# Query, gate and probability scratch tensors laid out by query block, compressed product last, rope query stores in one piece of 128 rows

## The chip, the cores and the metric

The kernel runs on one core of a Trainium2 chip, as one program and one launch. The metric is the device time of one execution in microseconds. A core has a matmul engine (PE, TensorE, with its weight loads as PEld), a vector engine (DVE), an activation engine (ACT), a general engine (POOL, GpSimd) and a queue engine (SP, SyncE) that issues nearly all transfers between DRAM and the on-chip memory. 16 DMA engines carry those transfers. PE writes its results to PSUM banks; DVE and ACT take them from there.

## The reference, cut to what matters

A trunk of two layers over a sequence of 1024 tokens. The second ("odd") layer mixes two attentions, and only its parts are touched here. NSA has 8 query heads on 2 key heads and adds three branches: compressed keys, selected blocks, and a window; MLA has 8 heads with a 64-wide plain part and a 32-wide rope part.

```python
def nsa_mixer(q, kv, gate_logits, ...):
    p_c = masked_softmax(s_c, dist_c >= 0)                       # compressed branch
    o_cmp = jnp.einsum('bygsc,bcyd->bsygd', p_c, vc)
    _, sel_idx = lax.top_k(sel_score, n_top)                     # blocks for the selected branch
    ...                                                          # o_sel, o_win by blocks of 128 queries
    o = g[:, :, 0] * o_cmp + g[:, :, 1] * o_sel + g[:, :, 2] * o_win

def mla_mixer(c_q, c_kv, k_rope, ...):
    q = (rms_norm(c_q, q_norm) @ w_uq).reshape(bsz, s_len, 8, 64 + 32)
    q = concat([q[..., :64], rope(q[..., 64:], positions)], -1)
    return einsum(masked_softmax(q @ k.T * scale), v)            # per head, causal

def odd_mixer(...):
    y_c = nsa_mixer(...) * jax.nn.silu(g_n)
    y_d = mla_mixer(...) * jax.nn.silu(g_m)
    return concat([y_c, y_d]) @ w_out
```

## The kernel before

All matrix products run on PE. A float32 operand is split into a high and a low part ("hi", "lo"), and three products are summed (`mm3`). A projection gives a PSUM tile `S` of 128 features x 1024 tokens (two of these exist, "banks" below); ACT and DVE take it out.

The second layer (`layer1`) runs these stages. `query_proj` makes the NSA queries: per head one tile `hp` of 128 rows (64 hi, 64 lo) x 1024 tokens, stored to `q_dram` (L1140). `cmp_attn` is the compressed branch in eight steps of 128 queries: softmax on DVE and ACT, then the probabilities, transposed, as `pcT` to `pc_dram` (L1191), and from step 4 on the block selection, stored as `sel_dram` (L1220). `gate_proj` makes the two gates (L1231, L1232) and stores them to `gn_dram` and `gm_dram` (L1233). `mla_q` makes the MLA queries in two rope parts (c = 0, 1: L1429 to L1438) and four plain parts (L1445 to L1451); both rope parts work in the same two halves of the tile `cst` (t1, t2), so that the second part may write them only when the stores of the first have landed. The rope store (L1438) goes to `qr_dram` as 4 heads x 32 rows x 1024, three times: hi, hi, lo.

Then `nsa` takes the query blocks of 128 in the order 1, 2, 0, 3, 4, 5, 6, 7. Its `load` brings a block's queries (L1299, L1301), the slope rows (L1302, on POOL), the selection rows (L1304), and gate and compressed probabilities into one tile `sgpc` (L1306, L1307). Two query slots are filled ahead, so the loads of the third block (i = 0) wait until the first block's last product has read its slot. Per block there are two head pairs `gp`; for each, one PSUM tile `o` (a single one exists) collects the compressed product (L1322), then the window and the selected branch (scores L1340, L1345, softmax L1241 to L1253, transposes L1265, products L1360), and `store_y` (L1280) takes it out. `mla` does the same for 16 steps of MLA; `mla_load` brings its queries (L1517, L1520, L1522).

The code is written in program order, and a scheduler of the framework decides in which order each engine's queue holds the instructions; so moving one statement changes the order of others. SP works its queue strictly in order. In the DRAM layouts of before, a tensor has one row per feature over all 1024 tokens, and a load of one block of 128 tokens therefore picks pieces of 128 float32 = 512 bytes; the stores write whole rows of 4 KB.

Of the kernel before, what the change touches and what calls it, by code (L numbers as in the profile page):

```python
# [6 lines left out]
F32 = mybir.dt.float32  # L7
# [15 lines left out]
class Trunk:  # L23
# [1127 lines left out]
    def cmp_attn(self):  # L1151
# [3 lines left out]
        self.pc_dram = self.dram.tile([8, 128, 4, 128], F32, name="pc_dram")  # L1155
# [11 lines left out]
        for i in range(8):  # L1167
# [23 lines left out]
            nc.sync.dma_start(self.pc_dram[i], pcT)  # L1191
            if i >= 4:
# [24 lines left out]
                sl = self.t4([2, 4, 128], F32R, name="sl")[0:16]  # L1217
                src = pt[0:16, 0:256].rearrange("p (y o t) -> p y o t", y=2, o=1).to_broadcast([16, 2, 4, 128])
                nc.scalar.copy(sl, src)
                nc.sync.dma_start(self.sel_dram[i - 4].bitcast(F32), sl.rearrange("p y g t -> p (y g) t").bitcast(F32))  # L1220
            yield

    def gate_proj(self, dst, cols):

        nc = self.nc
        for c2 in range(2):
            wt = self.wchunk(*cols(2 * c2), *cols(2 * c2 + 1))
            for cc in range(2):
# [4 lines left out]
                nc.sync.dma_start(dst[2 * c2 + cc], th)  # L1233
# [51 lines left out]
    def nsa(self):  # L1285
# [7 lines left out]
        src = self.q_dram.rearrange("h p t -> p h t")  # L1293

        def load(step):
# [10 lines left out]
            nc.sync.dma_start(sp[:, 0], self.gn_dram[:, :, ts].rearrange("g p t -> p g t"))  # L1306
            nc.sync.dma_start(sp[:, 1], self.pc_dram[i])  # L1307
# [6 lines left out]
        for step, i in enumerate(order):  # L1314
# [4 lines left out]
            for gp in range(2):  # L1319
                o = self.ps_o.tile([128, 2, 128], F32, tag="o", name="o")  # L1320
                for y in range(2):
                    nc.tensor.matmul(o[64 * y:64 * y + 64].rearrange("p g t -> p (g t)"), self.vc[64 * y:64 * y + 64],  # L1322
                                     pcT[64 * y:64 * y + 64, 2 * gp:2 * gp + 2].rearrange("p g t -> p (g t)"),
                                     start=True, stop=False, skip_group_check=True)
                for br, (KA, KB) in ((1, self.Kwin), (0, self.Ksel)):
# [5 lines left out]
                    for s0 in range(0, 4, hg):  # L1331
                        S = self.bank2().rearrange("p (h n) -> p h n", h=hg)
                        for s_ in range(hg):
                            y, g2 = divmod(s0 + s_, 2)
                            hd = 4 * y + 2 * gp + g2
# [22 lines left out]
                    for kt in range(nk):  # L1358
                        for y in range(2):
# [3 lines left out]
                                             start=False, stop=(br == 0 and kt == nk - 1), skip_group_check=True)  # L1363
# [32 lines left out]
    def mla_q(self):  # L1396
# [43 lines left out]
        for c in range(4):  # L1440
# [9 lines left out]
            for b in range(2):  # L1450
                nc.sync.dma_start(dst[192 * b:192 * b + 64], hi[64 * b:64 * b + 64].bitcast(F32))  # L1451
# [222 lines left out]
```

## Time and profile before

| what | value |
|---|---|
| three runs before | 1593.4, 1596.39, 1603.84 us; median 1596.39 |
| the profiled execution, its own time | 1592.17 us |
| its span in the trace | 1590.1 us |
| PE busy | 1475.7 us, 93% of the span |
| DVE, ACT, POOL busy | 993.7, 633.3, 369.5 us |
| chain that ended last | PE 70%, DVE 17%, issue 4%, DMA 3% |
| mean granted TensorE clock | 0.969 of full speed |

The profile is one execution. The span runs from the first to the last instruction; the execution's own time is 2.1 us longer. Times within the trace are counted from the span's start. A "releaser" is what ended an engine's idle time. The granted clock is given as a share of 2.4 GHz; 0.50 is the lower level, 1.2 GHz.

### The profile page before, as it was taken

The page shows a single profiled execution, that of the slowest core. Times are in us where ns is not written, and L with a number is a line of the kernel's source. Part 1 is how long each engine was busy: PE and PEld are TensorE (multiplying, and loading weights), DVE is VectorE, ACT ScalarE, POOL GpSimd, SP SyncE. Part 2 cuts the span into 40 slices and gives each one's busy share as a digit, 9 for nine tenths or more (in the row PEclk, how much of TensorE's full clock was granted, in tenths as well). Part 3 has the DMA queues.
Part 4 walks back from the last instruction along what each step waited for, and adds up shares of the span by engine and source line. Part 5 has one row for each costly group of instructions (what it writes and reads, how often), then busy time and mean ns, then how long its engine had stood idle before and what let it go on. Part 6 is the DMA issues. An engine that isn't in the chain of part 4 may idle for free.

```text
span 1590.1 us, 22273 instructions
## 1 busy us (share of the span) xinstructions
PE 1475.7 (93%) x8284; PEld 1176.6 (74%) x8284; DVE 993.7 (62%) x2168; ACT 633.3 (40%) x1293; POOL 369.5 (23%) x324
## 2 busy tenths in 40 slices
PE   4799999969899999999999979999999999998998
PEld 4597787757787788789877756666666777786787
DVE  6899999967544654661386336767775677544322
ACT  5332121247422343431253216767666666412211
POOL 4527733340323301410321300000001100223300
PEclk8899999979999999999999989999999999999999
DMA  8012453322522521542733246212113341532421
GB/s 251 14 53 81 126 180 131 127 73 79 184 99 80 179 98 66 148 144 82 185 92 103 77 133 192 70 51 61 36 45 89 86 124 52 149 110 80 160 86 69
DMA packets 144349, 168.65 MB, mean 106 GB/s; under 512 B 19817, under 2 KB 111713, under 8 KB 144241
## 3 DMA queue, kind: packets, MB, share of 16 engines
q1 hardware_dynamic: 139536, 155.83, 31.6%
q0 software_dynamic: 4544, 11.38, 2.5%
q8 instruction: 66, 1.08, 0.3%
q14 instruction: 43, 0.34, 0.1%
q10 hardware_dynamic: 160, 0.01, 0.0%
HBM read 114.20 MB, written 50.99 MB: 104 GB/s over the span
## 4 chain that ended last, share of the span: by engine, by line
PE 70%; DVE 17%; issue 4%; DMA 3%; ACT 2%; SPq 2%; POOL 2%; ACTq 0%; POOLq 0%; DVEq 0%
PE S L114 38%; PE tr L1265 7%; PE o L1360 5%; DVE conv L264 5%; PE tr L114 3%; PE o L1562 3%; PE S L1345 2%; PE S L1340 2%; PE S L1553 1%; PE S L1550 1%; PE tr L802 1%; PE S L1554 1%; PE S L1270 1%; SPq L1301 1%; PE tr L973 1%
## 5 line engine op out<-in xcount | busy, mean ns | idle before, releaser
L114 PE MATMUL S<-xT,wt 128*128 128x512 f32 x768 | 188.3, 401 | 4.2 <-DVE ext L249 4.2
L114 PE MATMUL S<-X,wt 128*128 128x512 f32 x768 | 185.2, 396 | 6.0 <-ACT wt L107 2.3
L114 PE MATMUL S<-wg,hT 128*128 128x512 f32 x720 | 176.8, 402 | 10.3 <-ACT wg L107 4.5
L114 PE MATMUL S<-wo,Y 128*128 128x512 f32 x768 | 181.5, 395 | 4.9 <-DVE gb L688 3.5
L114 PEld LDWEIGHTS S<-xT,wt 128*128 128x128 f32 x768 | 144.9, 192 | 35.6 <-DVE ext L249 5.0
L114 PEld LDWEIGHTS S<-X,wt 128*128 128x128 f32 x768 | 142.9, 189 | 37.4 <-issue 4.0
L114 PEld LDWEIGHTS S<-wo,Y 128*128 128x128 f32 x768 | 143.9, 189 | 35.8 <-DVE gb L688 3.9
L114 PEld LDWEIGHTS S<-wg,hT 128*128 128x128 f32 x720 | 136.7, 193 | 42.9 <-ACT wg L107 7.6
L1241 DVE TENSOR_REDUCE nm<-S 128x1 f32<-128x640 f32 (+7 forms) x132 | 129.2, 980 | 54.4 <-PE S L1345 34.4
L264 DVE SCALAR_TENSOR_TENSOR conv<-ext,conv 128x1024 f32<-128x1024 f32 x116 | 148.9, 1284 | 2.3
L108 POOL TENSOR_TENSOR wt<-raw,wt 128x1024 fp32r<-128x1024 f32 x34 | 82.5, 2442 | 115.4 <-ACT wt L107 115.2
L1244 ACT ACTIVATE pslot<-S,nm 128x640 f32<-128x640 f32 (+7 forms) x128 | 89.8, 709 | 25.6 <-DVE nm L1241 14.6
L1266 ACT COPY PT<-tr 128x512 f32<-128x512 f32 (+3 forms) x172 | 80.1, 491 | 45.6 <-PE tr L1265 42.5
L1265 PE MATMUL tr<-ident,pslot 128*128 128x128 f32 x528 | 84.7, 284 | 0.0
L1360 PE MATMUL o<-PT,vslot 128*64 128x256 f32 x528 | 84.5, 391 | 0.0
L1265 PEld LDWEIGHTS tr<-ident,pslot 128*128 128x128 f32 x528 | 58.6, 142 | 29.8 <-issue 20.8
L97 DVE TENSOR_SCALAR rs_v<-ss 128x1 f32<-128x1 f32 x32 | 4.9, 153 | 119.1 <-ACT lh L93 99.3
L1345 PE MATMUL S<-kst,qslot 112*128 112x512 f32 (+3 forms) x192 | 73.7, 396 | 0.0
L1340 PE MATMUL S<-kst,qslot 128*128 128x512 f32 (+3 forms) x192 | 69.7, 363 | 2.3 <-ACT pslot L1244 1.4
L787 POOL TENSOR_TENSOR lh<-lh 128x1024 f32<-128x1024 f32 x16 | 39.9, 2495 | 119.4 <-DVE lh L786 96.7
L93 ACT ACTIVATE lh<-S 128x1024 f32<-128x1024 f32 x16 | 16.4, 1026 | 123.6 <-issue 95.0
L852 DVE SCALAR_TENSOR_TENSOR ov<-ov,S 128x1024 f32<-128x1024 f32 (+1 forms) x17 | 19.7, 1157 | 72.3 <-issue 44.6
(433 smaller groups left out, 2812.5 us busy)
## 6 DMA issues: line engine op xcount, KB each, us to landing
h_dram<-lh POOLq DMA_DIRECT2D x16, 512.0 KB, 3.2
hr<-h_dram SPq DMA_DIRECT2D x14, 512.0 KB, 3.3
raw<-ev_w_in SPq DMA_DIRECT2D x16, 256.0 KB, 4.8
raw<-ev_w_in SPq DMA_DIRECT2D x8, 512.0 KB, 6.7
raw<-ev_w_out SPq DMA_DIRECT2D x8, 512.0 KB, 4.5
t<-ple_gate SPq DMA_DIRECT2D x8, 512.0 KB, 6.0
raw<-ple_gate SPq DMA_DIRECT2D x8, 512.0 KB, 5.9
lh<-x SPq DMA_DIRECT2D x8, 512.0 KB, 3.9
```

The source lines that it names most:

```text
L108: (eng or self.nc.gpsimd).tensor_tensor(lo, raw, hi, OP.subtract)
L114: self.nc.tensor.matmul(ps, l, r, start=n == 0, stop=n == len(seq) - 1)
L264: nc.vector.scalar_tensor_tensor(out=last if s == 30 else acc, in0=src, scalar=wc, in1=acc, op0=OP.mult, op1=OP.add)
L787: nc.gpsimd.tensor_tensor(hv, hv, xr, OP.add)
L1241: nc.vector.tensor_reduce(out=nm[:, 0:hg], in_=S[:, :, 0:n], op=OP.max, axis=AX.X, negate=True)
L1244: nc.scalar.activation(out=P[:, h, 0:n], in_=S[:, h, 0:n], func=AF.Exp, bias=nm[:, h:h + 1], accum_out=sm[:, h:h + 1])
L1265: nc.tensor.transpose(ps[:, c:c + 128], P[:, h, 128 * (k0 + k):128 * (k0 + k) + 128], self.ident)
L1266: nc.scalar.copy(PT[:, k0:k0 + n, s0:s0 + hg], ps[:, 0:128 * n * hg].rearrange("p (k h t) -> p k h t", h=hg, t=128))
L1340: nc.tensor.matmul(o_, QA[:, hd], KA[:, y, ks], start=True, stop=False)
L1345: nc.tensor.matmul(o_, qb[:, hd], KB[:, y, ks], start=False, stop=True)
L1360: nc.tensor.matmul(o[64 * y:64 * y + 64].rearrange("p g t -> p (g t)"), self.vsw[:, k0 + kt, 128 * br + 64 * y:128 * br + 64 * y + 64], PT ...
L1562: nc.tensor.matmul(o[64 * b:64 * b + 64, q], vm[:, kt, vs], PT[:, kt, 2 * b + q], start=(kt == 0), stop=(kt == nk - 1))
```

## The change

Four DRAM tensors get the query block i as first index: `q_dram` is [block, row, head, 128] instead of [head, row, 1024], `qm_dram` [block, half, row, head, 128], `gm_dram` [block, half, row, 2, 128], and `gp_dram` [block, row, 2, 4, 128] takes the place of `gn_dram` and `pc_dram`. A block's load then reads whole rows of 1, 2 or 4 KB, and the stores write pieces of 512 bytes. The heads are ordered by the half they belong to, so that the loads of halves are contiguous too; the slope rows come in two POOL transfers instead of one, the selection rows are stored in two halves from a tile of half the width, and gate and probabilities of a block come in one transfer. The plain MLA queries are stored in 16 transfers of 64 rows instead of 4 of 128 and 8 of 64. The rope queries are stored as 128 rows x 4 KB, once hi and once lo, and each MLA step reads them in three transfers of 32 rows. In `nsa` the compressed product comes after both branches instead of before.

```diff
@@ query_proj
-        self.q_dram = self.dram.tile([8, 128, 1024], F32R, name="q_dram")
+        self.q_dram = self.dram.tile([8, 128, 8, 128], F32R, name="q_dram")
...
-                    nc.sync.dma_start(self.q_dram[hd].bitcast(F32), A.bitcast(F32))
+                    nc.sync.dma_start(self.q_dram[:, :, 4 * b + c].rearrange("i p t -> p i t").bitcast(F32),
+                                      A.rearrange("p (i t) -> p i t", i=8).bitcast(F32))
@@ cmp_attn
-            nc.sync.dma_start(self.pc_dram[i], pcT)
+            nc.sync.dma_start(self.gp_dram[i, :, 1], pcT)
...
-                sl = self.t4([2, 4, 128], F32R, name="sl")[0:16]
+                sl = self.t4([2, 2, 128], F32R, name="sl")[0:16]
...
+                for b in range(2):
+                    nc.sync.dma_start(self.sel_dram[i - 4, :, 4 * b:4 * b + 4].bitcast(F32),
+                                      sl.rearrange("p y g t -> p (y g) t").bitcast(F32))
@@ gate_proj
-                nc.sync.dma_start(dst[2 * c2 + cc], th)
+                nc.sync.dma_start(dst(2 * c2 + cc), th.rearrange("p (i t) -> p i t", i=8))
@@ nsa, load
-            nc.sync.dma_start(QA.bitcast(F32), src[:, :, ts].bitcast(F32))
+            nc.sync.dma_start(QA.bitcast(F32), self.q_dram[i].bitcast(F32))
             for b in range(2):
-                nc.sync.dma_start(qb[0:64, b:8:2].bitcast(F32), src[64 * b:64 * b + 64, b:8:2, ts].bitcast(F32))
-            nc.gpsimd.dma_start(qb[64:66], d["c_qaug"][:, :, ts])
+                hs = slice(4 * b, 4 * b + 4)
+                nc.sync.dma_start(qb[0:64, hs].bitcast(F32), self.q_dram[i, 64 * b:64 * b + 64, hs].bitcast(F32))
+                nc.gpsimd.dma_start(qb[64:66, hs], d["c_qaug"][:, b:8:2, ts])
...
-            nc.sync.dma_start(sp[:, 0], self.gn_dram[:, :, ts].rearrange("g p t -> p g t"))
-            nc.sync.dma_start(sp[:, 1], self.pc_dram[i])
+            nc.sync.dma_start(sp, self.gp_dram[i])
@@ nsa, per head pair
-                for y in range(2):
-                    nc.tensor.matmul(o[64 * y:64 * y + 64]..., self.vc[64 * y:64 * y + 64], pcT[...], start=True, stop=False)
...
-                                             start=False, stop=(br == 0 and kt == nk - 1), skip_group_check=True)
+                                             start=(br == 1 and kt == 0), stop=False, skip_group_check=True)
+                for y in range(2):
+                    nc.tensor.matmul(o[64 * y:64 * y + 64]..., self.vc[64 * y:64 * y + 64], pcT[...], start=False, stop=True)
@@ mla_q
-        self.qr_dram = self.dram.tile([8, 96, 1024], F32R, name="qr_dram")
+        self.qr_dram = self.dram.tile([2, 2, 128, 1024], F32R, name="qr_dram")
...
-            for r, s in ((0, hi), (32, hi), (64, lo)):
-                nc.sync.dma_start(self.qr_dram[4 * c:4 * c + 4, r:r + 32].bitcast(F32), s.bitcast(F32))
+            for a, s in enumerate((hi, lo)):
+                nc.sync.dma_start(self.qr_dram[c, a].bitcast(F32), s.bitcast(F32))
...
             for b in range(2):
-                nc.sync.dma_start(dst[192 * b:192 * b + 64], hi[64 * b:64 * b + 64].bitcast(F32))
+                pr = slice(64 * b, 64 * b + 64)
+                dst = self.qm_dram[:, c // 2, :, 2 * b + c % 2].rearrange("i p t -> p i t").bitcast(F32)
+                for rows, s in ((pr, hi), (slice(64 - 64 * b, 128 - 64 * b), lo)):
+                    nc.sync.dma_start(dst[rows], s[pr].rearrange("p (i t) -> p i t", i=8).bitcast(F32))
@@ mla_load
-        nc.sync.dma_start(QR.bitcast(F32), self.qr_dram[hs, :, ts].rearrange("h p t -> p h t").bitcast(F32))
+        for r, a in ((0, 0), (32, 0), (64, 1)):
+            src = self.qr_dram[u, a, :, ts].rearrange("(h r) t -> r h t", h=4)
+            nc.sync.dma_start(QR[r:r + 32].bitcast(F32), src.bitcast(F32))
```

How the change moves instructions, as the built programs hold them. A row gives the line, the operation, the tile written and read, the shape, and a count. In the changed program the lines are some higher (L1442 is the rope store, L1301 and L1304 the query loads, L1309 the `sgpc` load, L1338 the first score product, L1363 the compressed product, L1456 the plain query store).

First, SP's queue where `mla_q`'s first rope part (`cst`) is stored and the first two query blocks (`qslot`, `sgpc`) are loaded, before:

```order
L1438 DMA qr_dram<-cst 4x32x1024 x3
L1299 DMA qslot<-q_dram 128x8x128
L1301 DMA qslot<-q_dram 64x4x128 x2
L1299 DMA qslot<-q_dram 128x8x128
L1301 DMA qslot<-q_dram 64x4x128 x2
L1306 DMA sgpc<-gn_dram 128x4x128
L1307 DMA sgpc<-pc_dram 128x512
```

The same place in the changed program:

```order
L1442 DMA qr_dram<-cst 128x1024
L1301 DMA qslot<-q_dram 128x1024
L1304 DMA qslot<-q_dram 64x512
L1442 DMA qr_dram<-cst 128x1024
L1304 DMA qslot<-q_dram 64x512
L1301 DMA qslot<-q_dram 128x1024
L1304 DMA qslot<-q_dram 64x512 x2
L1309 DMA sgpc<-gp_dram 128x1024 x2
```

Two rope stores stand where three stood, and the lo store has moved behind the first two loads.

Second, PE's queue between the last gate projection (`X`, `wt`) and the first NSA scores (`kst`, `qslot`); `Cq`, `wuq` is the MLA query projection, 12 rows to each of its parts. Before:

```order
L114 MATMUL S<-X_4694,wt 128x512 x4
L114 MATMUL S<-X_4695,wt 128x512 x4
L114 MATMUL S<-Cq,wuq 128x512 x36
L1322 MATMUL o<-sgpc,vc 64x256 x2
L114 MATMUL S<-Cq,wuq 128x512 x36
L1340 MATMUL S<-kst,qslot 128x256
```

Changed:

```order
L114 MATMUL S<-X_4694,wt 128x512 x4
L114 MATMUL S<-X_4695,wt 128x512 x4
L114 MATMUL S<-Cq,wuq 128x512 x72
L1338 MATMUL S<-kst,qslot 128x256
L1273 LDWEIGHTS mbf
L1273 MATMUL S<-mbf 128x128
```

The compressed product of the first head pair has left the middle of the MLA projection.

Third, SP's queue where the plain MLA queries (`hps`) are stored, ahead of the loads of the third query block, in the changed program:

```order
L1456 DMA qm_dram<-hps 64x8x128 x2
L1442 DMA qr_dram<-cst 128x1024
L1456 DMA qm_dram<-hps 64x8x128 x2
L1442 DMA qr_dram<-cst 128x1024
L1456 DMA qm_dram<-hps 64x8x128 x12
L1304 DMA qslot<-q_dram 64x512
L1301 DMA qslot<-q_dram 128x1024
```

Before, the same stretch held eight stores of 64 rows x 4 KB, four of 128 rows x 4 KB and three rope stores; the load of the third block stood behind them too.

## Rows read from the trace of the kernel before

**Rows 1.** Page, section 1: busy time, share, instructions of the engines.

```profile
PE 1475.7 (93%) x8284; PEld 1176.6 (74%) x8284; DVE 993.7 (62%) x2168; ACT 633.3 (40%) x1293; POOL 369.5 (23%) x324
```

**Rows 2.** Busy by stretch; the last three: granted clock, DMA share, GB/s.

```profile
core 0: us, PE busy (x) PEld busy (x) DVE busy (x) ACT busy (x) POOL busy (x), PEclk, DMA share, GB/s
918.00:934.00 16.00, 16.00 (x72) 13.14 (x70) 4.88 (x4) 2.09 (x2) 3.33 (x6) 1.00 0.35 113
934.00:946.00 12.00, 5.70 (x14) 3.80 (x12) 3.74 (x4) 1.06 (x2) 0.00 (x0) 0.72 0.49 151
946.00:962.00 16.00, 11.34 (x46) 8.64 (x47) 4.73 (x4) 3.49 (x4) 0.00 (x0) 0.79 0.59 182
968.00:980.00 12.00, 12.00 (x79) 8.70 (x78) 8.97 (x27) 9.08 (x31) 1.11 (x4) 0.86 0.78 221
980.00:1200.00 220.00, 220.00 (x1492) 143.73 (x1492) 160.28 (x386) 154.48 (x394) 7.44 (x14) 1.00 0.22 60
1260.00:1380.00 120.00, 118.85 (x992) 93.62 (x991) 80.44 (x164) 77.56 (x171) 10.53 (x7) 1.00 0.36 105
```

**Rows 3.** PE in order of time: start, duration, instruction, idle before and its releaser.

```profile
928.69 5.66 PE L114 MATMUL S<-Cq,wuq 128*128 128x512 f32 x24
939.33 5.36 PE L114 MATMUL S<-Cq,wuq 128*128 128x512 f32 x12 [4.99 <-DVE cst L1429]
950.66 1.12 PE L1322 MATMUL o<-sgpc,vc 64*64 64x256 f32 x4 [5.96 <-DMA sgpc<-pc_dram]
951.71 9.84 PE L114 MATMUL S<-Cq,wuq 128*128 128x512 f32 x36
961.39 0.28 PE L1340 MATMUL S<-kst,qslot 128*128 128x256 f32 x1
...
998.59 0.31 PE L1340 MATMUL S<-kst,qslot 128*128 128x128 f32 x1
```

**Rows 4.** DVE and ACT in order of time, the MLA query parts.

```profile
929.95 1.22 DVE L1232 SCALAR_TENSOR_TENSOR th<-th,S 128x1024 f32<-128x1024 f32 x1 [7.13 <-ACT th L1231]
938.05 1.22 DVE L1429 TENSOR_TENSOR cst<-S,cst 128x1024 f32<-128x1024 f32 x1 [6.88 <-DMA qr_dram<-cst]
943.45 1.22 DVE L1431 TENSOR_TENSOR cst<-S,cst 128x1024 f32<-128x1024 f32 x1 [4.17 <-DMA qr_dram<-cst]
944.73 1.02 ACT L1445 ACTIVATE hps<-S 128x1024 fp32r<-128x1024 f32 x1 [14.82 <-PE S L114]
```

**Rows 5.** SP's queue in order of time: start, time the issue took.

```profile
921.58 3.01 SPq L1438 DMA_DIRECT2D qr_dram<-cst  x3
924.70 3.87 SPq L1299 DMA_DIRECT2D qslot<-q_dram  x1
928.62 11.16 SPq L1301 DMA_DIRECT2D qslot<-q_dram  x2
...
954.27 1.13 SPq L1451 DMA_DIRECT2D qm_dram<-hps  x2
...
982.44 2.27 SPq L1301 DMA_DIRECT2D qslot<-q_dram  x1
```

**Rows 6.** Stretches, columns as in rows 2: rope stores; 4 KB; 512 B stores.

```profile
932.00:940.00 8.00, 3.01 (x13) 2.15 (x12) 1.22 (x1) 0.00 (x0) 0.00 (x0) 0.85 0.27 106
740.00:744.00 4.00, 4.00 (x21) 3.31 (x19) 1.23 (x1) 0.83 (x2) 0.00 (x0) 1.00 0.65 262
164.00:165.00 1.00, 1.00 (x6) 0.83 (x5) 1.00 (x3) 0.00 (x0) 0.39 (x1) 1.00 0.92 278
```

**Rows 7.** Transfers: count, KB each, median us from issue to landing.

```profile
CA_dram<-s5c SPq DMA_DIRECT2D x16, 128.0 KB, 2.4
gm_dram<-th SPq DMA_DIRECT2D x4, 512.0 KB, 2.6
```

**Rows 8.** POOL in order of time, and the slope rows' transfers from 915 to 960.

```profile
924.71 1.25 POOL L1302 DMA_DIRECT2D qslot<-c_qaug  x2
...
qslot<-c_qaug POOLq DMA_DIRECT2D x2, 8.0 KB, 8.7
```

**Rows 9.** ACT in order of time, with SP's query stores of that place.

```profile
796.25 1.98 ACT L107 CAST wt<-raw 128x1024 fp32r<-128x1024 f32 x2
798.25 1.02 ACT L1120 ACTIVATE hp<-S 64x1024 fp32r<-64x1024 f32 x1
...
791.71 6.24 SPq L1140 DMA_DIRECT2D q_dram<-hp  x3
```

**Rows 10.** Line L1522, the rope query loads of `mla`, and `store_y`'s L1280.

```profile
L1522 SPq DMA_DIRECT2D qmslot<-qr_dram x16: 543/544/601, 1187.0 to 1334.5; - x16
DMA to landing us min/median/max: 2.7/3.0/3.6
...
L1280 DVE SCALAR_TENSOR_TENSOR yt<-o,sgpc x16: 416/424/425, 977.7 to 1212.7; 128x256 f32<-128x256 f32 x16
```

**Rows 11.** Tile `sl`, the selection rows' copy on ACT.

```profile
L1219 ACT CAST sl<-tr x4: 1002/1002/1002, 854.5 to 892.4; 16x1024 fp32r<-16x1024 f32 x4
```

More of the change, by code (lines that the diff above doesn't have):

```diff
@@ L1154, in cmp_attn @@
         nc, d, V = self.nc, self.d, self.nc.vector
-        self.pc_dram = self.dram.tile([8, 128, 4, 128], F32, name="pc_dram")
         self.sel_dram = self.dram.tile([4, 16, 8, 128], F32R, name="sel_dram")
@@ L1334, in nsa @@
                             y, g2 = divmod(s0 + s_, 2)
-                            hd = 4 * y + 2 * gp + g2
+                            hd = 4 * g2 + 2 * y + gp
                             for c in range(0, n, 512):
@@ L1362, in nsa @@
                                              PT[:, kt, 2 * y:2 * y + 2].rearrange("p g t -> p (g t)"),
-                                             start=False, stop=(br == 0 and kt == nk - 1), skip_group_check=True)
+                                             start=(br == 1 and kt == 0), stop=False, skip_group_check=True)
+                for y in range(2):
+                    nc.tensor.matmul(o[64 * y:64 * y + 64].rearrange("p g t -> p (g t)"), self.vc[64 * y:64 * y + 64],
+                                     pcT[64 * y:64 * y + 64, 2 * gp:2 * gp + 2].rearrange("p g t -> p (g t)"),
+                                     start=False, stop=True, skip_group_check=True)
                 if i == 7 and gp == 0:
@@ L1423, in mla_q @@
         yield
-        self.qm_dram = self.dram.tile([8, 128, 1024], F32R, name="qm_dram")
-        self.qr_dram = self.dram.tile([8, 96, 1024], F32R, name="qr_dram")
+        self.qm_dram = self.dram.tile([8, 2, 128, 4, 128], F32R, name="qm_dram")
+        self.qr_dram = self.dram.tile([2, 2, 128, 1024], F32R, name="qr_dram")
         for c in range(2):
@@ L1536, in mla @@
             sgm = self.t2([2, 128], name="sgm")
-            nc.sync.dma_start(sgm, self.gm_dram[2 * u:2 * u + 2, :, ts].rearrange("g p t -> p g t"))
+            nc.sync.dma_start(sgm, self.gm_dram[i, u])
             hg = self.group_size(n)
@@ L1549, in mla @@
                         o_ = S[:, s_, ks]
-                        nc.tensor.matmul(o_, QA[:, h4], KA[:, h4, ks], start=True, stop=False)
+                        nc.tensor.matmul(o_, QA[:, s0 + s_], KA[:, h4, ks], start=True, stop=False)
                         if c + m == n:
                             self.add_mask(S[:, s_, n - 128:n], self.mask_diag)
-                        nc.tensor.matmul(o_, QB[:, h4], KB[:, q, ks], start=False, stop=False)
+                        nc.tensor.matmul(o_, QB[:, s0 + s_], KB[:, q, ks], start=False, stop=False)
                         nc.tensor.matmul(o_, QR[:, h4], KR[:, ks], start=False, stop=True)
@@ L1571, in layer1 @@
         w = self.d["od_w_in"][0]
-        self.gn_dram = self.dram.tile([4, 128, 1024], F32, name="gn_dram")
-        self.gm_dram = self.dram.tile([4, 128, 1024], F32, name="gm_dram")
+        self.gp_dram = self.dram.tile([8, 128, 2, 4, 128], F32, name="gp_dram")
+        self.gm_dram = self.dram.tile([8, 2, 128, 2, 128], F32, name="gm_dram")
         self.compress_in()
@@ L1587, in layer1, with gn, gm @@
         self.key_stacks()
-        for dst, cols in ((self.gn_dram, lambda k: [w[:, 1304 + 256 * y + 64 * k:1304 + 256 * y + 64 * k + 64]
-                                                    for y in range(2)]),
-                          (self.gm_dram, lambda k: [w[:, 2232 + 128 * k:2232 + 128 * k + 128]])):
-            if dst is self.gm_dram:
+        def gn(k):
+            return self.gp_dram[:, :, 0, k].rearrange("i p t -> p i t")
+        def gm(k):
+            return self.gm_dram[:, k // 2, :, k % 2].rearrange("i p t -> p i t")
+        for dst, cols in ((gn, lambda k: [w[:, 1304 + 256 * y + 64 * k:1304 + 256 * y + 64 * k + 64] for y in range(2)]),
+                          (gm, lambda k: [w[:, 2232 + 128 * k:2232 + 128 * k + 128]])):
+            if dst is gm:
                 mq = self.mla_q()
@@ L1595, in layer1 @@
                 next(cmp, None)
-                if dst is self.gm_dram and k in (2,3):
+                if dst is gm and k in (2,3):
                     next(mq)
```

14 lines of the change are left out of this document (3 added, 11 removed).

## The prediction

> **What bounds the kernel now.** I read the busy table first: PE is busy 93% of the span, no other engine over 62% [rows 1]. So a change counts where PE waits or runs slowly, and I looked for that by stretches. In the NSA stage (980 to 1200) PE is busy 220.00 of 220 us at full clock, in the main part of MLA 118.85 of 120 [rows 2]: there a faster transfer has nothing to give. Between 934 and 962, though, PE is busy only 5.70 of 12 and 11.34 of 16 us, at clock 0.72 and 0.79 [rows 2]. This is the passage from the last gate to the first NSA scores, and every part of the change meets in it.
>
> The order of time on PE shows two waits there [rows 3]. At 934.35 (928.69 + 5.66) PE has done both products of the second rope part and wants a free bank; it waits 4.99 us for L1429 on DVE. At 944.69 it has done the first plain part and comes to the compressed product L1322; it waits 5.96 us for the load of `pc_dram`. Behind each wait the clock is down: 12 products take 5.36 us where 24 took 5.66 before.
>
> What is late behind the two waits? L1429 starts at 938.05, after 6.88 us of waiting for the rope stores, and L1431 waits for them again [rows 4]. SP's queue says the same: it hands out three rope stores at 921.58, then the first query load takes 3.87 us to issue and the next two 11.16 us [rows 5]; the `sgpc` loads stand behind these. While SP hangs, the 16 DMA engines are only 27% busy and move 106 GB/s [rows 6], about a quarter of them. So it is not a shortage of bandwidth: the rope store, whose target begins with 4 heads, runs on about 4 engines. Three stores of 0.524 MB at 106 GB/s are 14.8 us, 921.6 to 936.4, close to where L1429 is let go.
>
> **The change part by part, here.** Rope stores: two instead of three, and 128 rows of 4 KB like the gate's store, which lands in 2.6 us [rows 7]. Issued at 921.6, hi has landed by about 924.2; lo is issued behind two loads, by about 925, and has landed by 928. Both are far ahead of DVE's needs (931.5, 934.4). Now the passage again, with 2.83 us for 12 products at full clock (half of 5.66), 1.02 us on ACT and 1.22 on DVE for each part [rows 3, 4]:
> the first rope product ends at 931.5, DVE has finished with the gate (929.95 + 1.22), L1429 runs 931.5 to 932.8, and its bank is free when PE asks at 934.35. Plain part 0 runs to 937.2, part 1 to 940.0. Part 2 needs the bank of part 0: ACT to 938.2, DVE to 939.4, in time; it runs to 942.8. Part 3 needs the bank of part 1: ACT to 941.0, DVE (behind the rope lo) to 942.3, in time; it runs to 945.6. The first scores need the bank of part 2: 942.8 + 1.02 + 1.22 = 945.1. So they start at 945.6 where they started at 961.39 [rows 3]: 15.8 us. By terms: 4.99 and 5.96 of waiting, 1.12 of the products L1322 that leave this place, 5.36 - 2.83 = 2.5 and 9.84 - 8.49 = 1.35 of half clock, 15.9 together.
>
> The products L1322 are moved, not removed. They come back inside the NSA stage, where PE has no gap: between 0.6 (half of 1.12, at full clock) and 1.12 us; I take 0.6. What remains is 15.2 us.
>
> Do the loads keep up with a start 15.8 us earlier? Two query blocks and two `sgpc` are 2 x (0.524 + 2 x 0.131) + 2 x 0.524 = 2.6 MB, with the rope stores 3.7 MB. At the rate of 4 KB rows (262 / 0.65 = 403 GB/s) that is 9 us, at that of 512 B pieces (278 / 0.92 = 302 GB/s) 12 us [rows 6]: done by 931 to 934, against 945.6. The slope rows are four POOL transfers instead of two: issued from 924.71 in 2.5 us instead of 1.25, landing 8.7 us later [rows 8], 936. Cover 10 us; without it each us late would be a us lost.
>
> **The other parts.** Stores in 512 B pieces: 0.524 MB takes 1.74 us instead of 1.30 by the two rates, 0.44 more. For the eight gate stores nothing waits (DMA share 0.35 and less around them [rows 2]). Of the query stores, three at 791.71 are slow already (6.24 us) and ACT's next `hp` at 798.25 reuses a buffer of the first [rows 9]; it could start 0 to 1.3 us later. I take 0. The selection copy is half as wide; four of 1.00 us [rows 11] give between 0 and 2 us on ACT. PE's waits in that stretch end on DVE, so I take 0.
>
> Plain query stores: 16 of 64 rows in 512 B pieces instead of 12, the same 4.19 MB. In SP's order the loads of the third block stand behind them. They begin at about 938 instead of 954.27; before, they and three rope stores kept SP until 982.44 [rows 5], 28 us. Even with 28 us the load starts at 966 and lands near 970; PE wants it at 998.59 - 15.8 = 982.8 [rows 3]. Cover 12 us: nothing.
>
> The compressed product last: `o` becomes free one product later, since `store_y` (0.42 us [rows 10]) can only follow it. A group's first product then comes at most 0.6 + 0.42 = 1.0 us too early, 16 times: 0 to 16 us. In the new queue two to eight transposes and mostly new scores stand between L1363 and the next group's first product, so I take 0.
>
> MLA: three rope loads of 32 rows a step instead of one: two more issues of 0.54 us on SP, landing 3.0 us [rows 10]. A step is over 7 us (120 us for some 14 steps [rows 2]), SP idles most of it, and the loads run a step ahead: nothing. The `qm`, `gm` and query loads in longer rows save DMA time that nobody waits for.
>
> **Sum.** 1592.2 - 15.8 + 0.6 = 1577.0 us against the profiled execution, a ratio of 0.990. That execution is 4.2 us below the median of the runs shown and 1.2 below the lowest. With the ratio the median 1596.4 becomes 1581.2. I forecast between the two: 1579 us.
>
> **Rivals.**
> *A wait stays in the passage* (1582 to 1587). If anything still holds PE 3 us at 934 (the rope lo, the bank order), the clock goes down again and part 0 costs 2.5 us more: 5.5 us less gain, 1582.5 on the profiled execution's scale, up to 1587 on that of the runs. For it: three engines have to mesh within a margin of 0.3 to 1.6 us, as worked out above. Against: all of these margins are small only beside PE work, and a miss costs its own size.
>
> *The NSA order costs what the passage gives* (1583 to 1592). The scheduler has reordered the whole stage. If `o` really stands between the groups, the 1.0 us of each of 16 groups returns and the time is 1592. For it: PE had no gap, so each new one is loss. Against: DVE is busy 160 and ACT 154 of 220 us [rows 2], so both have room, and the amount of work is the same.
>
> *The plain query stores come late* (slower, 1593 to 1612). A store of 64 rows and 128 KB lands in 2.4 us when alone [rows 7]; twice the bytes take at most 4.8. One after another, 16 would take 77 us, from 938 to 1015, the load of block 0 would land at 1018 instead of 982.8, and PE would wait 35 us: 1577 + 35 = 1612. It decides from (982.8 - 3.3 - 938) / 16 = 2.6 us for each store; at 3.6 us the whole gain is gone. Against: the 28 us above are a bound of 2.3 us for each twelfth part of the same bytes, with rope stores on top, at 221 GB/s [rows 2].
> The Trainium skill ("DMA: Bandwidth & Descriptors", section "Rules for kernel authors") speaks for this rival: two transfers to disjoint halves of the partitions serialize, and one transfer of 128 should be used instead; by it the sixteen halves would run as sixteen transfers in a row, which is the case just priced. No run here shows two such halves apart; I give it the small chance that the 28 us leave.
>
> *More comes back* (1570 to 1574). The clock of 968 to 980 is 0.86 [rows 2], 1.7 us; with the 2 us of the selection copy the time is 1573. Against: the fill of the softmax pipeline that lowers the clock there stays.
>
> **How the numbers follow.** Forecast 0.61 (its own range 1574 to 1584), a wait stays 0.14, the NSA order 0.13, late stores 0.06, more 0.06. The range 1570 to 1590 leaves out the late stores and the worst of the NSA order, about 0.1. A change of about 1% is what a measurement of this kernel can tell from none, here 1580.4 against 1596.4. The forecast lies on this border: I put 0.65 of it below (0.40), and with the case "more" faster has 0.46. Slower is the late stores, 0.06. The rest, 0.48, is within 1%.
>
> **What would show it.** Right: no wait of PE for L1433 (the old L1429) nor for `sgpc`, the first scores near 946, the clock 1.00 from 918 on, DMA share well over 0.27 while rope stores run, SP's query loads issued in under 1 us each; NSA still 220 us from block 1's end to block 7's. Wrong: PE waiting at the scores of the third block on `qslot` (the late stores), PE gaps before a group's first L1358 (the NSA order), or a first score near 950 (a wait stays).

## The result, and the profile after

The changed kernel takes 1579.34 us (median; 1576.96 to 1583.41) where the kernel before takes 1594.99 beside it (four runs, three of them those shown ahead of the prediction). The ratio on record is 0.9877, interval 0.9844 to 0.9911; the quotient of the two medians, 0.9902, lies inside it. Measured once more beside the last experiments it is 0.9892 (0.9863 to 0.992). The profiled execution takes 1576.96 us with a span of 1575.2.

The stretches of [rows 2] again, after (columns as there; the last one holds work that stood some 15 us later before):

```profile
core 0: us, PE busy (x) PEld busy (x) DVE busy (x) ACT busy (x) POOL busy (x), PEclk, DMA share, GB/s
918.00:934.00 16.00, 16.00 (x72) 13.18 (x71) 6.79 (x6) 2.09 (x2) 4.35 (x8) 1.00 0.80 237
934.00:946.00 12.00, 12.00 (x55) 9.86 (x54) 7.25 (x6) 4.03 (x4) 0.00 (x0) 1.00 0.80 242
946.00:962.00 16.00, 13.72 (x92) 10.73 (x92) 11.34 (x24) 10.33 (x36) 1.63 (x5) 0.89 0.91 232
980.00:1200.00 220.00, 218.46 (x1501) 145.36 (x1500) 155.87 (x363) 152.44 (x382) 13.95 (x22) 1.00 0.19 54
```

From 934 to 946 PE is now busy 12.00 of 12 us at clock 1.00 (before: 5.70 at 0.72), and the DMA share from 918 to 946 is 0.80. The order of time on PE, which answers to [rows 3]:

```profile
918.87 11.05 PE L114 MATMUL S<-X,wt 128*128 128x512 f32 x48
929.75 16.59 PE L114 MATMUL S<-Cq,wuq 128*128 128x512 f32 x72
946.18 0.28 PE L1338 MATMUL S<-kst,qslot 128*128 128x256 f32 x1
...
948.72 0.38 PE L1338 MATMUL S<-kst,qslot 128*128 128x256 f32 x1 [0.92 <-DVE hps L1450]
...
951.81 0.38 PE L1338 MATMUL S<-kst,qslot 128*128 128x256 f32 x1 [1.37 <-ACT pslot L1247]
...
959.27 0.42 PE L1338 MATMUL S<-kst,qslot 128*128 128x384 f32 x1
```

All six remaining query parts (72 products) run in one piece, and the first scores follow at 946.18. SP's queue, after, which answers to [rows 5]:

```profile
922.66 0.34 SPq L1442 DMA_DIRECT2D qr_dram<-cst  x1
923.60 0.34 SPq L1301 DMA_DIRECT2D qslot<-q_dram  x1
...
925.70 1.26 SPq L1301 DMA_DIRECT2D qslot<-q_dram  x1
927.01 1.36 SPq L1304 DMA_DIRECT2D qslot<-q_dram  x2
928.42 1.06 SPq L1309 DMA_DIRECT2D sgpc<-gp_dram  x2
...
941.63 2.85 SPq L1456 DMA_DIRECT2D qm_dram<-hps  x2
...
945.87 14.46 SPq L1456 DMA_DIRECT2D qm_dram<-hps  x12
960.43 1.02 SPq L1304 DMA_DIRECT2D qslot<-q_dram  x1
```

The first two `sgpc` loads are out by 929.48; the plain query stores keep SP until 960.33, and the load of block 0 follows at once, 22 us before PE comes to that block's scores (982.78). On DVE the first rope product of the second part waits for PE alone, no longer for a transfer as in [rows 4]:

```profile
932.68 1.23 DVE L1433 TENSOR_TENSOR cst<-S,cst 128x1024 f32<-128x1024 f32 x1 [0.44 <-PE S L114]
935.45 1.23 DVE L1435 TENSOR_TENSOR cst<-S,cst 128x1024 f32<-128x1024 f32 x1 [1.54 <-PE S L114]
```

**How the runs are compared.** Single executions of one kernel lie up to 15 us apart (e4: 1586.98 to 1602.38 in ten runs; before: 1591.72 to 1605.34 in 22). In the traces much of that comes ahead of the change: the last gate product, a run of 48 products, starts at 914.84 in one trace and at 922.05 in another of kernels whose code is the same up to there (e11, e6). The passage behind it, from the start of that product to the first NSA scores, repeats to 0.02 us in four profiles (the changed kernel twice, e8, e9); each kernel in which PE waits there has one profile. So each profile is cut into three: the start of that product, the passage, and what is left from the first scores to the end of the span (us). The ratio in the last column is to runs of the kernel before beside it.

| kernel | gate product starts | passage | rest | time as a ratio to before |
|---|---|---|---|---|
| before | 917.78 | 43.61 | 628.71 | 1 |
| changed | 918.87 | 27.31 | 629.02 | 0.9877 (0.9844 to 0.9911) |
| changed, again | 923.61 | 27.31 | 630.68 | 0.9892 (0.9863 to 0.992) |
| e1 before, rope store of 128 rows | 917.21 | 29.90 | 630.99 | 0.9914 (0.9882 to 0.9947) |
| e2 before, compressed product last | 915.29 | 35.27 | 631.84 | 0.9952 (0.9925 to 0.9978) |
| e3 block layout alone | 918.54 | 42.64 | 629.02 | 0.9962 (0.994 to 0.9983) |
| e4 changed, old rope store | 921.63 | 34.63 | 638.84 | 0.9978 (0.9954 to 1.0002) |
| e5 changed, compressed product first | 916.04 | 28.19 | 628.57 | 0.9904 (0.9883 to 0.9926) |
| e6 before, two pieces of 4 x 32 | 922.05 | 41.75 | 627.10 | 0.9981 (0.9963 to 0.9999) |
| e7 before, three pieces of 128 | 920.84 | 28.16 | 629.00 | 0.9891 (0.9871 to 0.991) |
| e8 changed, query stores of 128 rows | 914.45 | 27.29 | 630.16 | one execution, 1573.65 us |
| e9 changed, one rope load a step | 919.61 | 27.29 | 631.10 | 0.9891 (0.9859 to 0.9922) |
| e10 changed, last query part between scores | 917.45 | 24.56 | 629.99 | 0.985 (0.9821 to 0.988) |
| e11 before, rope stores from ScalarE's queue | 914.84 | 42.90 | 629.26 | 0.9982 (0.9964 to 1.0) |

In e10 one query part of 2.7 us stands behind the first scores, so its passage is shorter by that without a gain.

### The profile page after: what moved, and what is told of

It reads as the page before. It is cut to its first block, busy times and chain, and to the rows that moved or that the text cites. A ratio compares the mean times of both kernels' runs of the same rounds, so it can differ in the third digit from the quotient of the medians.

```text
span 1575.2 us, 22336 instructions
## 1 busy us (share of the span) xinstructions
PE 1467.4 (93%) x8284; PEld 1172.2 (74%) x8284; DVE 998.9 (63%) x2168; ACT 631.0 (40%) x1293; POOL 372.9 (24%) x332
## 4 chain that ended last, share of the span: by engine, by line
PE 67%; DVE 20%; issue 4%; ACT 3%; DMA 2%; POOL 2%; SPq 1%; ACTq 0%; POOLq 0%; DVEq 0%
PE S L114 37%; DVE conv L264 7%; PE tr L1268 6%; PE o L1358 5%; PE tr L114 3%; PE o L1568 2%; PE S L1343 2%; PE S L1338 2%; PE S L1559 1%; PE S L1556 1%; PE tr L802 1%; PE S L1560 1%; PE S L1273 1%; PE tr L973 1%; DVE s5a L507 1%
## 5 line engine op out<-in xcount | busy, mean ns | idle before, releaser
L1268 PEld LDWEIGHTS tr<-ident,pslot 128*128 128x128 f32 x528 | 58.4, 142 | 24.9 <-issue 19.6
L1338 PE MATMUL S<-kst,qslot 128*128 128x512 f32 (+3 forms) x192 | 69.7, 363 | 3.5 <-ACT pslot L1247 2.5
L852 DVE SCALAR_TENSOR_TENSOR ov<-ov,S 128x1024 f32<-128x1024 f32 (+1 forms) x17 | 19.7, 1157 | 72.1 <-issue 44.6
```

Of the source, the lines that this page charges most:

```text
L1268: nc.tensor.transpose(ps[:, c:c + 128], P[:, h, 128 * (k0 + k):128 * (k0 + k) + 128], self.ident)
L1338: nc.tensor.matmul(o_, QA[:, hd], KA[:, y, ks], start=True, stop=False)
```

## The experiments: one part of the change at a time

**e1, the rope store alone.** The kernel before, with

```diff
-            for r, s in ((0, hi), (32, hi), (64, lo)):
-                nc.sync.dma_start(self.qr_dram[4 * c:4 * c + 4, r:r + 32].bitcast(F32), s.bitcast(F32))
+            for a, s in enumerate((hi, lo)):
+                nc.sync.dma_start(self.qr_dram[c, a].bitcast(F32), s.bitcast(F32))
...
```

The lines that lay `qr_dram` out and load it to match are left out here, and in e6 and e7 below.

> The kernel before with one part of the change: the rope query store in two pieces of 128 rows, loaded in three pieces of 32 rows. Theory (the shape of the rope store causes both waits of the passage, the second one because it keeps SP's queue shut in front of the loads of queries and gates): both waits go, the first NSA scores start near 946 instead of 961.4, the time falls by 14 to 16 us, to about 1580 where the kernel before has 1595. Rival A (the second wait has its own cause, the product that stands first and the load it needs): only 4.99 us and 2.5 us of half clock go, the second wait of some 6 us stays, about 1587.

PE in order of time, e1:

```profile
928.11 5.62 PE L114 MATMUL S<-Cq,wuq 128*128 128x512 f32 x24
935.50 0.65 PE L1322 MATMUL o<-sgpc,vc 64*64 64x256 f32 x4 [1.77 <-DMA sgpc<-pc_dram]
936.08 11.19 PE L114 MATMUL S<-Cq,wuq 128*128 128x512 f32 x48
947.11 0.28 PE L1340 MATMUL S<-kst,qslot 128*128 128x256 f32 x1
```

13.7 of the 16.3 us come from this part alone. The first wait is gone, the second shrinks from 5.96 to 1.77 us: it hung on the rope store, not on a cause of its own. What is left of it goes with the order: the scheduler put the compressed product behind 24 products here, where 36 stood ahead of it before [rows 3]. In e7 below, with 36 ahead again, it waits for nothing.

**e2, the compressed product alone** (the two products L1322 behind both branches, `start` on the first product of the window branch).

> The kernel before with one part of the change: the compressed product behind both branches. Theory: the wait for the rope store stays (4.99 us, half clock behind it); the wait of 5.96 us for the gates leaves PE, which fills it with the plain query parts until about 954; first scores near 954 to 955, 0.6 us come back in the NSA stage: about 1589. Rival A (each wait has its own cause): about the same, 1588 to 1589, which makes e1 the run that decides. Rival B (the block layout opens the queue): PE meets the query loads next, 1593 to 1595.

The wait for L1429 stays, and the passage is 8.3 us shorter (PE in order of time, e2):

```profile
936.65 4.96 PE L114 MATMUL S<-Cq,wuq 128*128 128x512 f32 x12 [4.83 <-DVE cst L1429]
942.26 8.46 PE L114 MATMUL S<-Cq,wuq 128*128 128x512 f32 x36 [0.65 <-DVE cst L1431]
950.56 0.28 PE L1336 MATMUL S<-kst,qslot 128*128 128x256 f32 x1
```

**e3, the block layout alone** (the changed kernel with the old rope store and the old place of the product).

> The changed kernel without its rope store (three pieces of 4 x 32 rows again, one load of 96 rows) and with the compressed product first again: what is left is the block layout of queries, gates and probabilities. Theory: next to nothing, since SP is still shut behind the rope stores: 1593 to 1596, PE still waits some 5 us for the first rope part and some 5 us for the gates. Rival B (longer rows in the loads open SP's queue): the waits of SP on the query loads (3.87 and 11.16 us) shrink, 1582 to 1587.

Both waits stay, and the passage is only 1.0 us shorter (PE, then SP's queue):

```profile
939.97 5.43 PE L114 MATMUL S<-Cq,wuq 128*128 128x512 f32 x12 [4.88 <-DVE cst L1433]
949.51 1.12 PE L1324 MATMUL o<-sgpc,vc 64*64 64x256 f32 x4 [4.11 <-DMA sgpc<-gp_dram]
```

```profile
929.48 2.96 SPq L1304 DMA_DIRECT2D qslot<-q_dram  x2
...
938.59 5.23 SPq L1309 DMA_DIRECT2D sgpc<-gp_dram  x2
```

The half of rival B that speaks of SP came true: the six query loads take SP 9.2 us to hand out instead of 19.7 (the pair at 929.48 takes 2.96 instead of 11.16). Its gain did not: the `sgpc` loads go out at 938.59 and take 5.23 us themselves, and the gates are there 31.0 us behind the start of the gate product instead of 32.9 (949.51 - 918.54, 950.66 - 917.78). By time e3 is 0.9962, with an interval below 1, 4.6 us between the medians; 1.0 us of that lies in the passage, and where the rest lies the runs do not show. e2 and e3 together with e1 add up to 23 us where the whole change has 16.3: they are different ways around the same obstacle.

**e4, the changed kernel without its rope store** (the three pieces of 4 x 32 rows again).

> The changed kernel with only the rope store as it was (three pieces of 4 x 32 rows, one load of 96 rows). Theory: as e2, the first wait and its half clock are back, the second is not: 1588 to 1590, 9 to 10 us over the changed kernel. Rival A: the same 1587 to 1589. Rival B (the block layout carries the gain): 1579 to 1582.

The passage is 7.3 us longer than the changed kernel's, as expected, but the rest is 8 to 10 us longer too, and the gain is all but gone (0.9978). SP and PE say why (SP's queue; PE; the stretch behind PE's wait, columns as in [rows 2]):

```profile
956.79 3.69 SPq L1442 DMA_DIRECT2D qr_dram<-cst  x3
960.54 29.55 SPq L1456 DMA_DIRECT2D qm_dram<-hps  x14
990.19 1.08 SPq L1304 DMA_DIRECT2D qslot<-q_dram  x1
```

```profile
996.95 0.44 PE L1338 MATMUL S<-kst,qslot 128*128 128x128 f32 x1 [5.41 <-DMA qslot<-q_dram]
```

```profile
997.00:1005.00 8.00, 8.00 (x38) 6.41 (x40) 2.79 (x9) 2.75 (x13) 0.19 (x1) 0.51 0.48 130
```

Fourteen query stores take 29.55 us here, 2.1 us each; the same fourteen take 17.31 in the changed kernel (2.85 and 14.46), 1.2 each. The difference is 12.2 us; three rope stores need 14.8 us at 106 GB/s. So the load of block 0 goes out at 990.19 instead of 960.43, and PE waits 5.41 us for it. Behind the wait the clock is 0.51 for 8 us, which is about 4 us more; together that is the 8 to 10 us. The rival of the late query stores named this outcome, but by another cause: here rope stores slow the query stores, not the halves each other. The changed kernel is kept from it by its rope store alone.

**e5, the changed kernel with the product first.**

> The changed kernel with the compressed product ahead of both branches again. Theory: with the rope store out of the way the gates land near 932, before PE has done the second rope part, so the product waits for nothing; it takes 0.6 us in the passage and 0.6 less later: as the changed kernel within 1 us, 1578 to 1581. In the part without the block layout (e1) the wait was still 1.8 us, so up to 1.8 us is left open. Rival (the order of the product is what removes the second wait): a wait of 4 us or more for the gates, 1584 to 1588.

The product waits for nothing; the passage is 0.9 us longer, the rest shorter by 0.5 and 2.1 us than in the two profiles of the changed kernel. Once the rope store is right, the place of the product is worth nothing that these runs can tell. What the product at the end costs can be read from the waits of PE (us in total, times, longest), e5, then the changed kernel:

```profile
PE S L1342 <- ACT pslot L1247: 1.4, 1, 1.4
```

```profile
PE S L1338 <- ACT pslot L1247: 2.5, 5, 1.4
```

## The experiments: the rope store's shape, count and queue

**e6, two pieces in the old shape**, and **e7, three pieces in the new shape**, both on the kernel before:

```diff
-            for r, s in ((0, hi), (32, hi), (64, lo)):
+            for r, s in ((0, hi), (32, lo)):
...
```

```diff
-            for r, s in ((0, hi), (32, hi), (64, lo)):
-                nc.sync.dma_start(self.qr_dram[4 * c:4 * c + 4, r:r + 32].bitcast(F32), s.bitcast(F32))
+            for a, s in enumerate((hi, hi, lo)):
+                nc.sync.dma_start(self.qr_dram[c, a].bitcast(F32), s.bitcast(F32))
...
```

> The kernel before with two rope stores instead of three, in their old shape of 4 x 32 rows (the high part is loaded twice). Theory (the shape is slow): 106 GB/s as before, 1.05 MB take 9.9 us instead of 14.8, the passage shrinks by about 5 us, the wait for the gates is still there: 1588 to 1592. Rival (the third piece, its bytes and its place in the queue, is the cause): both waits go as in e1, 1580 to 1584.

> The kernel before with three rope stores of 128 rows each (the high part is still written twice): only the shape is changed, neither the count nor the bytes. Theory: as e1 plus at most 1.3 us, 1580 to 1585, the DMA engines move over 250 GB/s while the stores run. Rival (count and bytes): as before within 4 us, 1591 to 1597.

Stretches while the rope stores run, e6, then e7:

```profile
932.00:936.00 4.00, 4.00 (x19) 3.30 (x18) 1.22 (x1) 1.03 (x1) 0.00 (x0) 1.00 0.38 103
```

```profile
926.00:932.00 6.00, 6.00 (x28) 4.95 (x28) 0.00 (x0) 0.09 (x1) 3.03 (x5) 1.00 0.96 311
```

One third of the bytes less in the old shape brings 1.9 us, not the 5 expected. The gates do come 4.8 us earlier: they are there 28.1 us behind the start of the gate product, before 32.9 (950.14 - 922.05, 950.66 - 917.78). But in this kernel's order the compressed product stands right behind the rope part, with 24 products ahead of it instead of 36. The wait for L1429 no longer shows on PE; PE waits 11.56 us for the gates in one piece, and the twelve products that it did in that time before now stand behind it (12.77 us, before 9.84 [rows 3]):

```profile
950.14 1.12 PE L1322 MATMUL o<-sgpc,vc 64*64 64x256 f32 x4 [11.56 <-DMA sgpc<-pc_dram]
951.19 12.77 PE L114 MATMUL S<-Cq,wuq 128*128 128x512 f32 x48
```

All the bytes in the new shape bring 15.4 us and 0.9891, nearly the 16.3 us of the whole change, and the compressed product waits for nothing, e7:

```profile
940.12 0.65 PE L1322 MATMUL o<-sgpc,vc 64*64 64x256 f32 x4
```

So the shape is the cause; the third piece costs something only in the old shape. e5, which is e7 with two pieces and the block layout, has the same passage (28.19 and 28.16 us): with the shape right, layout and third piece are worth nothing there.

The packet records of the traces bear on how many engines a store has. From 932 to 940 in the kernel before, only the rope stores move packets of 4 KB. Four of these are under way at once for 84% of that time, with a median of 159 ns each, and 4 x 4096 bytes in 159 ns are 103 GB/s. In e7, from 926 to 932, the commonest number is sixteen. The Trainium skill ("DMA: Bandwidth & Descriptors", section "Why a DMA increments its semaphore by 16 and not by 1") has it that a transfer runs on the largest number of engines up to 16 that divides the slowest dimension of both sides, which makes 4 for a target of 4 x 32 x 1024 and 16 for 128 x 1024. These counts agree, and so do 106 GB/s at a share of 0.27 before (4.3 of 16 engines) and 311 GB/s at 0.96 in e7, loads included.

**e11, the rope stores from another queue.** The kernel before, with the three stores of 4 x 32 rows issued by ScalarE (`nc.scalar.dma_start`), nothing else.

> The kernel before with its three rope stores handed out by ScalarE's queue instead of SP's, shape and count as before. Theory (SP is shut because the stores stand ahead of the loads in its own queue): SP issues the query loads in under 1 us each, the gates land before 935, the second wait goes; the first wait stays, since DVE still waits for a store of 106 GB/s: 1586 to 1590. Rival (the engines that carry the rope store are full, and every load that has a share on them is late, whichever queue hands it out): the gates come as late as before, the second wait stays, 1593 to 1597.

SP's queue, then PE, e11:

```profile
920.00 7.89 SPq L1301 DMA_DIRECT2D qslot<-q_dram  x2
927.96 2.78 SPq L1299 DMA_DIRECT2D qslot<-q_dram  x1
930.80 8.89 SPq L1301 DMA_DIRECT2D qslot<-q_dram  x2
939.77 1.22 SPq L1306 DMA_DIRECT2D sgpc<-gn_dram  x1
```

```profile
937.73 4.34 PE L114 MATMUL S<-Cq,wuq 128*128 128x512 f32 x12 [6.34 <-DVE cst L1429]
947.22 1.12 PE L1322 MATMUL o<-sgpc,vc 64*64 64x256 f32 x4 [5.14 <-DMA sgpc<-pc_dram]
```

SP has no rope store ahead of its loads now and still hangs for 19.6 us on five of them. The `sgpc` loads stand behind these and go out at 939.77; the gates come as late as before, 32.4 us behind the start of the gate product (before 32.9). My theory that SP is shut because the stores stand ahead in its own queue falls, and what the rival forecast came: the loads are late whichever queue carries the stores. That they are late because they have a share on the engines that the rope stores fill fits this, but no run shows it apart; what in an engine holds them up stays open.

## The experiments: other doubts

**e8, query stores of 128 rows.**

```diff
-            for b in range(2):
-                pr = slice(64 * b, 64 * b + 64)
+            for b, s in enumerate((hi, lo)):
                 dst = self.qm_dram[:, c // 2, :, 2 * b + c % 2].rearrange("i p t -> p i t").bitcast(F32)
-                for rows, s in ((pr, hi), (slice(64 - 64 * b, 128 - 64 * b), lo)):
-                    nc.sync.dma_start(dst[rows], s[pr].rearrange("p (i t) -> p i t", i=8).bitcast(F32))
+                nc.sync.dma_start(dst, s.rearrange("p (i t) -> p i t", i=8).bitcast(F32))
```

> The changed kernel with eight plain query stores of 128 rows instead of sixteen of 64 rows, the same bytes and the same pieces of 512 bytes. The halves of the low part go to other rows than the loads expect, so the heads of MLA compute with permuted queries; the amount of work is the same. Theory (the pieces of 512 bytes set the rate, not the halves): SP needs as long for the eight as for the sixteen, 15 to 19 us, and they move 210 to 230 GB/s; the time is that of the changed kernel, 1576 to 1581. Rival (two halves run one after the other and one transfer of 128 rows would do both at once, as the Trainium skill has it): half of that, 8 to 10 us, at twice the rate; the time is the same there too, since the loads behind them have cover.

Stretches within the query stores, behind the last rope store, the changed kernel (64 rows), then e8 (128 rows):

```profile
950.00:960.00 10.00, 8.63 (x56) 7.04 (x54) 7.54 (x20) 7.13 (x28) 1.63 (x5) 0.83 0.94 227
```

```profile
943.00:949.00 6.00, 3.72 (x22) 2.94 (x21) 5.05 (x9) 3.62 (x15) 0.19 (x1) 0.80 1.01 287
```

The engines move 227 GB/s in halves and 287 in whole rows, a factor of 1.26. Neither expectation holds: the halves are not free, and whole rows are not twice as fast. 4.19 MB take 18.5 us by the one rate and 14.6 by the other; the passage is the same (27.31 and 27.29 us), so nobody there waits for the 3.9 us.

**e9, one rope load a step in MLA.**

> The changed kernel with the rope queries loaded in one piece of 96 rows a step, as before, instead of three of 32. The store is three whole pieces of 128 rows, one after the other in a store of 4 x 96 rows, so the load finds other rows than it should: the rope part of the MLA scores is computed with permuted values, the work is the same. Theory (the three loads cost what the first steps of MLA lost: PE waits 0.2 us for the load and runs at half clock for some 7 us from 1204.8 where the kernel before did so for some 3): 1 to 2 us between the first scores of NSA and the end, 1577 to 1579. Rival (the loss there is the softmax that fills its pipeline, whatever the loads): nothing, 1579 to 1581, the half clock lasts as long.

Nothing is gained. PE at the first long MLA scores, e9, then the changed kernel:

```profile
1207.01 0.41 PE L1555 MATMUL S<-KAm,qmslot 128*128 128x384 f32 x1 [2.30 <-DVE sr L1254]
1208.80 0.69 PE L1559 MATMUL S<-qmslot 96*128 96x384 f32 x1 [1.08 <-DMA qmslot<-qr_dram]
```

```profile
1204.77 0.44 PE L1556 MATMUL S<-KAm,qmslot 128*128 128x384 f32 x1 [2.14 <-DVE sr L1251]
1206.19 0.66 PE L1560 MATMUL S<-qmslot 96*128 96x384 f32 x1 [0.20 <-DMA qmslot<-qr_dram]
```

The wait ahead of them is there with one load as with three, and before the change too (2.73 us at the same scores). The half clock behind it lasts some 6 us in both. The three loads cost nothing that can be seen.

**e10, a version that goes further.** What is left of the passage are two waits, shown above for PE after the change: 0.92 us at the second scores, for DVE to take the last query part out, and 1.37 us at the third, for ACT's softmax. The last plain query part is put between the first and the second scores:

```diff
+                        if step == 0 and gp == 0 and br == 1:
+                            yield
...
+            yield
...
         next(nsa)
+        for _ in range(3):
+            next(mq)
+        next(nsa)
         self.run(mq)
```

> The changed kernel with the last plain query part between the first NSA scores and the second ones: nothing is left out, only the order in the program is another. Theory (what is left of the passage is the wait for the first softmax, 0.92 and 1.37 us and 4 us of half clock behind them): the part of 2.8 us fills it, 2 to 4 us less than the changed kernel, 1575 to 1577.5. Rival (the bank of the last part is needed by the second scores, and the wait only moves): within 1 us of the changed kernel.

```profile
942.01 0.28 PE L1338 MATMUL S<-kst,qslot 128*128 128x256 f32 x1
...
944.55 3.00 PE L114 MATMUL S<-Cq,wuq 128*128 128x512 f32 x12 [0.92 <-DVE hps L1452]
...
953.46 0.38 PE L1338 MATMUL S<-kst,qslot 128*128 128x256 f32 x1 [0.35 <-ACT pslot L1247]
...
955.81 0.42 PE L1338 MATMUL S<-kst,qslot 128*128 128x384 f32 x1
```

The 0.92 us only move, as the rival had it, and stand ahead of the query part now; of the 1.37 us 0.35 are left, and the half clock behind them is gone (1.00 from 950 to 960, where the changed kernel has 0.83). The first scores of 384 columns (the second query block) come 38.4 us after the start of the gate product (955.81 - 917.45) instead of 40.4 (959.27 - 918.87): 2.0 us. By time it is the best of the kernels with more than one run, 1573.77 us and 0.985 (0.9821 to 0.988); against the changed kernel's 0.9892 the intervals overlap a little, so it is the 2.0 us of the trace that I hold to.

**The changed kernel again.**

> The changed kernel once more, on the chip of these three, so that they can be compared with it: 1577 to 1582, first NSA scores 27 us after the start of the last gate product, 629 us from there to the end.

Passage 27.31 us, twice the same; start and rest differ by 4.7 and 1.7 us between the two profiles. That is what a single total here is worth.

## Why the prediction was right, point by point

**The place and the cause.** Right. Both waits went with the shape of the rope store alone (e7; e1 leaves 1.77 us of the second, by its order). The four engines, inferred from a share of 0.27, stand in the packet records. The second wait came about as written, too: SP hangs on the query loads, and the `sgpc` loads stand behind these. e11 has the same, without a rope store in SP's queue; what it refutes is the theory of e1 and e11, that SP hangs because the stores stand ahead in its own queue. One figure is too small: the three stores were to be done in 14.8 us, by 936.4, but DVE is let go by them at 938.05 and, for L1431, only at 943.45 [rows 4], 21.9 us after they were handed out. The sum does not use it; it took the waits as measured.

**The passage.** Forecast: first scores at 945.6 from a gate product at 917.78, 27.8 us. Measured 27.31. The term that was off is the 2.83 us for 12 products, half of a row of 24: six parts take 16.59 us in one row, 2.77 each. Bank after bank came free in the order worked out: L1433 and L1435 wait for PE, at 932.68 and 935.45 (forecast 931.5 and 934.4, with a start 1.1 us earlier). The clock, forecast as 1.00 from 918 on, is so up to 946; from 946 to 962, where PE waits 0.92 and 1.37 us at the second and third scores, it is 0.89.

**The loads.** Right in what matters: all are out by 929.5. "Under 1 us each" on SP was too bold, some take 1.26 us. The four slope transfers took POOL 2.27 us (forecast 2.5).

**The query stores.** Right for this kernel (load of block 0 at 960.43, forecast 966 at the latest; wanted at 982.78, forecast 982.8), but I called the cover 12 us without saying what it hangs on. The rival's price of 2.4 to 4.8 us for each store of 64 rows was too high: twelve take 14.46 us, 1.2 each. e4 shows that with slow rope stores among them the same stores eat the cover and 5.41 us more. A chance of 0.06 for late stores was fair for the change as a whole and not for its parts.

**What comes back.** Forecast 0.6 us. The four profiles with the product last and no other disturbance (the changed kernel twice, e8, e9) have a rest of 630.2 on average; the seven with it first (before, e1, e3, e5, e6, e7, e11) have 628.95. That is 1.3 us, with single values 627.1 to 631.1; the two profiles of the changed kernel alone differ by 1.7, so the 0.6 can neither be confirmed nor refuted. The extra short waits for ACT (2.5 against 1.4 us) would cover most of the difference, which is argued and not shown. `o` does not hold PE up at the groups: the longest wait at a product into it is 0.4 us, for the transposed probabilities, so that rival did not come.

**The total.** The sum said 1577.0 for the profiled execution, and it is 1576.96. By spans: 1590.1 + 1.09 (later start) - 16.30 + 0.31 = 1575.2. That it fits to a tenth is luck; the changed kernel's second profile has a span of 1581.6 with the same passage. The forecast of 1579 for the median, between the two scales, met 1579.34, within a scatter of several us. Whether the gain is above or below 1%, to which the chances gave 0.46 and 0.48, the interval (0.9844 to 0.9911) leaves open.

**MLA and the selection copy.** Taken as nothing, and nothing is seen. The four copies take 0.57 instead of 1.00 us, but PE waits as long between 780 and 916 us as before (8.1 and 8.0 us in all, 2.3 of it for ACT in both). In MLA, e9 gains nothing, and the wait at the first scores is 2.1 to 2.8 us in every profile, before and after. In the profile before and in the first of the changed kernel DVE ends it; in the second of the changed kernel a load of the plain queries does (2.5 us), so there these loads land late, which the forecast ("a step ahead") did not see; the wait is no longer by it.

## What to carry to other kernels

Look at the slowest dimension of a store's target: while stores to one that begins with 4 ran, the engines moved 103 to 106 GB/s, and 311 while stores to one that begins with 128 ran. The slow stores held up the loads beside them from either queue that was tried (e11). When a wait ends on a late load, ask first which other transfer holds the engines; a new order of the work (e2) or a better layout of the load (e3) then helps only around the obstacle. Check what an edit does to the order of the queues, too: e1 and e6 moved the compressed product ahead of twelve others without a word of it in their edits. And cut profiles at fixed work: the passage repeated to 0.02 us where totals lay up to 15 us apart.

## What the runs showed of the hardware that I had not expected

Pairs of loads on SP's queue took 7.89 and 8.89 us to issue with the slow stores on ScalarE's queue (e11). Pieces of 512 bytes moved at 227 GB/s from 64 rows and at 287 GB/s from 128 rows (e8). The Trainium skill ("DMA: Bandwidth & Descriptors", section "Rules for kernel authors") has it that two transfers to disjoint halves of the partitions serialize and that one of 128 should be used instead. e8 agrees with the advice, by a factor of 1.26; the page gives no factor, and the factor of two in the rival on record for e8 was my own reading of it. Three rope stores in the old shape lengthen the fourteen query stores behind them by 12.2 us (e4).
